# Modulation rows of a two-layer transformer formed on VectorE during the mixers, instead of on TensorE there and on VectorE in the first value stage

## The chip, the core and the metric

The kernel runs on one core of a Trainium2 chip. The metric is the device time of one execution in microseconds: the median of three executions of the kernel before is 2929.69 us, the lowest 2916.97 and the highest 2932.78.

## What is computed

Two layers over 256 context and 256 latent tokens of width 1024. In each layer six modulation vectors of length 1024 are formed for the latent stream (from c) and for the context stream (from c_ctx). They shift and scale two norms and gate two residuals:

```python
sh1, sc1, g1, sh2, sc2, g2 = jnp.split((jax.nn.silu(c) @ w_ada + b_ada)[:, None, :], 6, axis=-1)
h = rmsnorm(x, norm1_g) * (1.0 + sc1) + sh1
# four head groups on columns of h @ w_in: neighbourhood attention, mLSTM, latent attention, window attention
x = x + g1 * (jnp.concatenate([y_a, y_b, y_c, y_d], axis=-1) @ w_out)
h2 = rmsnorm(x, norm2_g) * (1.0 + sc2) + sh2
x = x + g2 * peer_ffn(h2, peer_wq, peer_keys, peer_u, peer_v)
```

`peer_ffn` routes each token to 128 of 16384 experts (8 heads, 16 each), takes gelu of its dot product with rows of `peer_u`, and sums gated rows of `peer_v`. In the second layer only the latent tokens go on after the mixers.

## The kernel before

Activations lie transposed, 128 features by 512 tokens in eight tiles. A product with a weight is three matmuls in fp32r (`mm3`, L72 to L74): the weight is loaded by SyncE's queue into a `raw` tile (2 buffers), split into a high part by ScalarE (L408) and a low part by VectorE (L412), and both parts go into `spl` tiles (10 buffers of 128x1024, taken in turn by everything that splits).

**Mixers** (`mixers`, from the start to about 455 us in layer 0 and from about 1800 to 2074 us in layer 1). TensorE's order is the order of the code. `run_units` walks over attention units, one per head and query tile of 128 tokens: 64 units in layer 0 (16 each of mLSTM, neighbourhood, latent and window attention), 32 in layer 1. For each unit it issues four transposes (`tp`, L611), the score of the unit two ahead (`sc`), then as filler some matmuls of the job list `F`, then the product with the values (`py`, L622) of the unit before, then filler again. The softmax of a unit is on VectorE and ScalarE between its score and its transposes: VectorE reduces the maximum (L567), ScalarE takes the exponential (L573), VectorE inverts the sum and scales (L577, L578). The filler jobs are the projections still needed (`naq`, `nak`, `cq`, `ckv`, `swq`, `swk`), then in layer 0 twelve jobs `ada8` to `ada19`, and, once the latent attention is done, the output projection `wo`. VectorE and ScalarE are ordered in this stretch by the framework's scheduler.

**Modulation.** Chunks 0 to 7 of layer 0 (first norm) are formed at the start on TensorE. Chunks 8 to 19 (rows 16 to 39: g1, sh2, sc2) are the twelve filler jobs (`ada_steps`): a load of 1 MB, four high and four low splits, 16 matmuls of 256 columns against `cs` (L260, L261), a copy by ScalarE (L267) and two small matmuls (L279, four records) that bring the row back. Everything else, rows 40 to 47 of layer 0 and all 48 of layer 1, is formed in the first value stage by `ada_row`: a load of 512 KB from `wadat`, two VectorE products of 128x1024 with a sum (L299, one for c, one for c_ctx, against `csb`, silu of c and c_ctx on every partition) and one small add (L300).

**Peer stage.** First norm and routing, then the `u` stage (64 pairs of blocks of experts, matmuls into `pu`), then the value stage (64 pairs, matmuls into `f`; 384 tokens in layer 0, 256 in layer 1). In layer 0 one tile of 128 tokens (`tokens_apart`) is not multiplied but gathered: GpSimd fetches rows, VectorE multiplies and adds them (L1363, L1370), spread over the `u` and the value stage. Each pair in the value stage needs four splits (L1447 on ScalarE, L1448 on VectorE) and the gated activations (L1453 to L1455). The last pair is written out by hand and begins with a lone L72 matmul.

Of the kernel before, what the change touches and what calls it, by code (L numbers as in the profile page):

```python
# [53 lines left out]
class Kernel:  # L54
# [33 lines left out]
    def build(self):  # L88
        tc, nc, A = self.tc, self.nc, self.A
        with ExitStack() as es:  # L90
# [26 lines left out]
            self.gd = [self.dram.tile([self.wd[l] // 32, 128, 128, 32], F32, name=f"gd{l}") for l in range(L)]  # L117
            self.ad = [self.dram.tile([128, 128, self.wd[l]], F32, name=f"ad{l}") for l in range(L)]
# [10 lines left out]
    def start(self):  # L129
# [15 lines left out]
        self.cs = self.sm.tile([128, KD, 128], F32R, name="cs", bufs=1)  # L145
        for half in range(2):
            zero = self.new()
            nc.gpsimd.memset(zero, 0.0)
            nc.scalar.copy(self.cs[:, 4 * half:4 * half + 4], zero.rearrange("p (a b) -> p a b", b=128))
        nc.vector.tensor_copy(self.cs[:, :, 0:2], cc)  # L150
        nc.vector.tensor_tensor(self.cs[:, :, 2:4], cc, self.cs[:, :, 0:2].bitcast(F32), op=ALU.subtract)
# [64 lines left out]
    def ada_full(self, raw, ch):  # L216
# [8 lines left out]
        row = self.sm.tile([4, 256], F32, name="adarow")  # L225
# [14 lines left out]
    def ada_parts(self, parts, ch):  # L240
        nc = self.nc
        ps = self.psc.tile([128, 512], F32, name="sc")
        for k in range(KD):
            c = slice(k % 2 * 256, k % 2 * 256 + 256)
            nc.tensor.matmul(ps[:, 0:256], self.cs[:, k, :], parts[k // 2][0][:, c], start=(k == 0), stop=False)
            nc.tensor.matmul(ps[:, 0:256], self.cs[:, k, :], parts[k // 2][1][:, c], start=False, stop=(k == KD - 1))
        self.ada_out(0, ch, ps)

    def adaload(self, l, ch):
        return self.wload(self.A["wada"][l, ch])  # L250

    def ada_steps(self, w, l, ch):

        nc = self.nc
        wh, wl = w
        if l not in self.mod:
            self.mod[l] = self.cst.tile([128, 6, KD, 2], F32, name=f"mod{l}")
        ps = self.psf.tile([128, 512], F32, name="fp")
        for k in range(KD):
            nc.tensor.matmul(ps[:, 0:256], self.cs[:, k, :], wh[:, k, :], start=(k == 0), stop=False)  # L260
            nc.tensor.matmul(ps[:, 0:256], self.cs[:, k, :], wl[:, k, :], start=False, stop=(k == KD - 1))  # L261
            yield 0.22
        self.ada_out(l, ch, ps)

    def ada_out(self, l, ch, ps):
        row = self.sm.tile([4, 256], F32, name="adarow")
# [17 lines left out]
    def ada_end(self):  # L284
        for _ in range(4):
            yield 0
        self.ada_turn()

    def ada_row(self, pool, l, n):

        nc = self.nc
        if l not in self.mod:
            self.mod[l] = self.cst.tile([128, 6, KD, 2], F32, name=f"mod{l}")
        s, k = divmod(n, KD)
        w = pool.tile([128, 1024], F32, name="adaw", bufs=2)
        nc.sync.dma_start(w, self.A["wadat"][l, n])
        for j in range(2):
            o = self.mod[l][:, s, k, j:j + 1]
            self.pin(nc.vector.scalar_tensor_tensor(self.junk, w, 1.0, self.csb[:, j], op0=ALU.mult, op1=ALU.mult, accum_out=o))  # L299
        nc.vector.tensor_add(self.mod[l][:, s, k], self.mod[l][:, s, k], self.badat[:, l, s, k:k + 1].to_broadcast([128, 2]))  # L300
# [124 lines left out]
    def mixers(self, l):  # L425
        tc, nc = self.tc, self.nc
        with ExitStack() as es:
# [37 lines left out]
            if l == 0:  # L465
# [115 lines left out]
    def run_units(self, units):  # L581
# [23 lines left out]
        for i, u in enumerate(units + [None]):  # L605
            if u is not None:
# [1142 lines left out]
```

## Time and profile before

| | |
|---|---|
| median of 3 executions | 2929.69 us |
| the profiled execution | 2918.53 us, span 2916.6 us |
| TensorE busy | 2789.8 us (96%), 18199 matmul records |
| VectorE busy | 2187.1 us (75%) |
| ScalarE busy | 1266.0 us (43%) |
| chain that ended last | TensorE 74%, VectorE 15%, DMA 3%, ScalarE 3% |
| mean granted clock | 0.981 |

A row of the profile names the line, the engine, the operation and its tiles (output<-inputs), then the count, the busy time and the mean of one in ns, then the idle time of the engine just before these instructions and what ended it. Matmuls are pipelined: the distance from one start to the next is what a matmul costs, not its shown length. PEld is TensorE's loading of weights. The granted clock is 1.00 at 2.4 GHz and 0.50 at 1.2 GHz.

### The profile page before, as it was taken

The page shows a single profiled execution, that of the slowest core. Times are in us where ns is not written, and L with a number is a line of the kernel's source. Part 1 is how long each engine was busy: PE and PEld are TensorE (multiplying, and loading weights), DVE is VectorE, ACT ScalarE, POOL GpSimd, SP SyncE. Part 2 cuts the span into 40 slices and gives each one's busy share as a digit, 9 for nine tenths or more (in the row PEclk, how much of TensorE's full clock was granted, in tenths as well). Part 3 has the DMA queues.
Part 4 walks back from the last instruction along what each step waited for, and adds up shares of the span by engine and source line. Part 5 has one row for each costly group of instructions (what it writes and reads, how often), then busy time and mean ns, then how long its engine had stood idle before and what let it go on. Part 6 is the DMA issues. An engine that isn't in the chain of part 4 may idle for free.

```text
span 2916.6 us, 47051 instructions
## 1 busy us (share of the span) xinstructions
PE 2789.8 (96%) x18199; PEld 2538.2 (87%) x18199; DVE 2187.1 (75%) x4703; ACT 1266.0 (43%) x2185; POOL 393.2 (13%) x354
## 2 busy tenths in 40 slices
PE   8999998999899997999999998999999999999998
PEld 5766777999888887999999997766899999999998
DVE  5664757679999985799999986654779767666665
ACT  5553634334344432343333334543545444444443
POOL 0110000002444433412222310000000000000000
PEclk9999999999999998999999999999999999999999
DMA  7210413326999999999999983211445766876774
GB/s 261 73 44 29 159 59 116 129 96 219 330 344 367 368 359 380 358 324 367 376 373 379 376 297 128 74 37 37 171 142 184 241 243 237 285 251 234 254 247 143
DMA packets 268752, 662.88 MB, mean 227 GB/s; under 512 B 16496, under 2 KB 146672, under 8 KB 258928
## 3 DMA queue, kind: packets, MB, share of 16 engines
q1 hardware_dynamic: 198688, 450.04, 44.1%
q0 software_dynamic: 36864, 134.23, 12.3%
q10 hardware_dynamic: 32976, 75.61, 6.8%
q8 instruction: 142, 2.33, 0.3%
q14 instruction: 82, 0.67, 0.1%
HBM read 585.37 MB, written 74.45 MB: 226 GB/s over the span
## 4 chain that ended last, share of the span: by engine, by line
PE 74%; DVE 15%; issue 4%; DMA 3%; ACT 3%; SPq 1%; POOL 0%; ACTq 0%; DVEq 0%; POOLq 0%
PE pu L72 8%; PE pu L74 8%; PE pu L73 8%; PE f L73 8%; PE f L74 7%; PE f L72 7%; PE fp L72 4%; PE fp L73 3%; PE fp L74 3%; PE py L622 3%; DVE spl L1448 2%; DVE junk L299 2%; PE pg L1328 2%; PE mm L72 2%; PE mm L73 2%
## 5 line engine op out<-in xcount | busy, mean ns | idle before, releaser
L72 PE MATMUL pu<-h2h,spl 128*128 128x384 f32 (+1 forms) x2048 | 647.9, 316 | 31.1 <-ACT spl L1396 30.0
L74 PE MATMUL pu<-h2h,spl 128*128 128x384 f32 (+1 forms) x2048 | 636.2, 312 | 10.1 <-DVE spl L1397 9.9
L73 PE MATMUL f<-wl,spl 128*128 128x384 f32 (+1 forms) x2048 | 634.0, 310 | 7.0 <-DVE wl L1455 7.0
L73 PE MATMUL pu<-h2l,spl 128*128 128x384 f32 (+1 forms) x2048 | 637.7, 311 | 0.0
L74 PE MATMUL f<-wh,spl 128*128 128x384 f32 (+1 forms) x2048 | 626.7, 309 | 0.0
L72 PE MATMUL f<-wh,spl 128*128 128x384 f32 (+1 forms) x2048 | 515.5, 311 | 9.6 <-ACT wh L1454 6.3
L1448 DVE TENSOR_TENSOR spl<-raw,spl 128x1024 fp32r<-128x1024 f32 x256 | 311.4, 1223 | 153.2 <-ACT spl L1447 151.8
L1447 ACT CAST spl<-raw 128x1024 fp32r<-128x1024 f32 x256 | 267.9, 1049 | 364.5 <-PE f L73 334.5
L72 PEld LDWEIGHTS pu<-h2h,spl 128*128 128x128 f32 x2048 | 391.5, 191 | 39.4 <-ACT spl L1396 35.6
L1396 ACT CAST spl<-raw 128x1024 fp32r<-128x1024 f32 x256 | 266.6, 1049 | 329.0 <-PE pu L73 227.3
L74 PEld LDWEIGHTS pu<-h2h,spl 128*128 128x128 f32 x2048 | 390.9, 191 | 15.3 <-DVE spl L1397 14.8
L73 PEld LDWEIGHTS f<-wl,spl 128*128 128x128 f32 x2048 | 388.9, 190 | 12.5 <-DVE wl L1455 11.1
L73 PEld LDWEIGHTS pu<-h2l,spl 128*128 128x128 f32 x2048 | 392.0, 191 | 0.4
L72 PEld LDWEIGHTS f<-wh,spl 128*128 128x128 f32 x2048 | 377.3, 190 | 15.9 <-ACT wh L1454 10.7
L1397 DVE TENSOR_TENSOR spl<-raw,spl 128x1024 fp32r<-128x1024 f32 x256 | 311.3, 1218 | 104.9 <-ACT spl L1396 94.6
L74 PEld LDWEIGHTS f<-wh,spl 128*128 128x128 f32 x2048 | 388.5, 190 | 0.0
L1414 ACT ACTIVATE act<-pu 128x384 f32<-128x384 f32 (+1 forms) x216 | 95.8, 443 | 232.3 <-PE pu L74 232.2
L412 DVE TENSOR_TENSOR spl<-raw,spl 128x512 fp32r<-128x512 f32 (+1 forms) x226 | 150.0, 699 | 58.9 <-ACT spl L408 47.9
L1454 ACT CAST wh<-va 128x384 fp32r<-128x384 f32 (+1 forms) x216 | 100.1, 467 | 185.3 <-DVE va L1453 77.6
L341 POOL TENSOR_TENSOR ms<-ms,mhalf 128x4 f32<-128x4 f32 (+1 forms) x5 | 4.8, 953 | 1300.6 <-DVE sq L339 834.0
L1357 POOL DMA_INDIRECT spl<-in_un,ix x92 | 125.0, 1359 | 393.5 <-DVE fp L1225 242.9
L408 ACT CAST spl<-raw 128x512 fp32r<-128x512 f32 (+1 forms) x226 | 130.7, 629 | 85.5 <-PE fp L73 44.2
(305 smaller groups left out, 4715.9 us busy)
## 6 DMA issues: line engine op xcount, KB each, us to landing
raw<-in_ut SPq DMA_DIRECT2D x128, 1024.0 KB, 5.3
raw<-in_v SPq DMA_DIRECT2D x128, 1024.0 KB, 5.6
adaw<-in_wadat SPq DMA_DIRECT2D x56, 512.0 KB, 7.5
ad<-act ACTq DMA_DIRECT2D x64, 384.0 KB, 5.1
gd<-gstage ACTq DMA_DIRECT2D x12, 2048.0 KB, 10.9
vg<-gd SPq DMA_DIRECT2D x32, 768.0 KB, 8.7
va<-ad SPq DMA_DIRECT2D x64, 384.0 KB, 7.6
raw<-in_win SPq DMA_DIRECT2D x22, 1024.0 KB, 4.9
```

What stands on the lines that cost most here:

```text
L72: mm(ps, ah, bh, start=first, stop=False, **kw)
L73: mm(ps, ah, bl, start=False, stop=False, **kw)
L74: mm(ps, al, bh, start=False, stop=last, **kw)
L408: return self.nc.scalar.copy(p[0][o], w[:, o])
L412: return eng.tensor_tensor(p[1][o], w[:, o], p[0][o].bitcast(F32), op=ALU.subtract)
L1357: nc.gpsimd.indirect_dma_start(r, None, tabs[which], bass.IndirectOffsetOnAxis(ix[:, s:s + 1], 0))
L1396: self.pin(nc.scalar.copy(uh, self.u[:, n % 2]), n < 3)
L1397: self.pin(nc.vector.tensor_tensor(ul, self.u[:, n % 2], uh.bitcast(F32), op=ALU.subtract), n < 3)
L1414: nc.scalar.activation(a[:, b, :w], ps[:, :w], AF.Gelu)
L1447: nc.scalar.copy(vh, v[:, b])
L1448: nc.vector.tensor_tensor(vl, v[:, b], vh.bitcast(F32), op=ALU.subtract)
L1454: nc.scalar.copy(wh[:, :w], a[:, b, :w])
```

## The change

The twelve filler jobs are gone. Rows 16 to 47 of both layers are formed on VectorE during the mixers: `run_units` takes one row after every second unit in layer 0 and after every unit in layer 1. In layer 1 only one product per row is made, since only the latent stream is left. Rows 0 to 15 of layer 1 stay in the first value stage, one after every third pair. The row's weights and the unused product go into two `spl` tiles. silu of c and c_ctx is formed once, early in the first mixers, and kept in DRAM (`csd`). To make room, `cs` moves into `s` tiles and two small pools shrink (`adarow` from 4 to 2 buffers, `dg` from 4 to 3).

```diff
+            self.csd = self.dram.tile([128, 2, 1024], F32, name="csd")
...
-        self.cs = self.sm.tile([128, KD, 128], F32R, name="cs", bufs=1)
+        self.cs = [self.new(F32R).rearrange("p (a b) -> p a b", b=128) for _ in range(2)]
...
-        row = self.sm.tile([4, 256], F32, name="adarow")
+        row = self.sm.tile([4, 256], F32, name="adarow", bufs=2)
...
+    def modulation(self, l):
+        nc = self.nc
+        nv = 2 if l == 0 else 1
+        self.csb = self.sm.tile([128, nv, 1024], F32, name="csb", bufs=1)
+        if l == 0:
+            nc.sync.dma_start(self.csb, self.A["ccb"])
+            for j in range(2):
+                sg = self.spl.tile([128, 1024], F32, name="spl")
+                nc.scalar.activation(sg, self.csb[:, j], AF.Sigmoid)
+                nc.vector.tensor_mul(self.csb[:, j], self.csb[:, j], sg)
+            nc.scalar.dma_start(self.csd, self.csb)
+        else:
+            nc.sync.dma_start(self.csb, self.csd[:, 0:1])
+        def rows():
+            for n in range(16, 48):
+                w, junk = (self.spl.tile([128, 1024], F32, name="spl") for _ in range(2))
+                self.ada_row(w, junk, l, n, nv)
+                yield
+        self.adarows = rows()
...
-            self.pin(nc.vector.scalar_tensor_tensor(self.junk, w, 1.0, self.csb[:, j], op0=ALU.mult, op1=ALU.mult, accum_out=o))
+            nc.vector.scalar_tensor_tensor(junk, w, 1.0, self.csb[:, j], op0=ALU.mult, op1=ALU.mult, accum_out=o)
...
-                for c in range(8, 20):
-                    F.add(f"ada{c}", lambda c=c: self.adaload(l, c), lambda w, c=c: self.ada_steps(w, l, c))
-                F.add("ada", None, lambda w: self.ada_end())
...
+            self.modulation(l)
             F.finish("mlg")
...
         for i, u in enumerate(units + [None]):
+            if (i + 1) * 32 // n > i * 32 // n:
+                next(self.adarows, None)
...
-                        extra = [(0, n) for n in range(40, 48)] + [(1, n) for n in range(48)]
+                        nc.sync.dma_start(self.csb, self.csd)
+                        extra = list(range(16))
...
-                        if extra:
-                            self.ada_row(self.vp, *extra.pop(0))
+                        if extra and n % 3 == 0:
+                            self.ada_row(self.vp.tile([128, 1024], F32, name="adaw", bufs=2), self.junk, 1, extra.pop(0), 2)
```

Two places of the built order matter. The first is TensorE's, in the second half of layer 0's latent attention. Before, after the score of a unit (six matmuls into `sc`), filler of the ada jobs follows:

```order
L261 MATMUL fp<-spl,cs 128x256
L611 MATMUL tp<-con,s 128x128 x4
L72 MATMUL sc<-s 128x512
L73 MATMUL sc<-s 128x512
L74 MATMUL sc<-s 128x512
L72 MATMUL sc<-s 128x512
L73 MATMUL sc<-s 128x512
L74 MATMUL sc<-s 128x512
L260 MATMUL fp<-spl,cs 128x256
L261 MATMUL fp<-spl,cs 128x256
```

With the change (lines are shifted by one) the score is followed at once by the values' product of the unit before:

```order
L722 MATMUL mm<-con,s 128x128 x4
L623 MATMUL py<-s 64x128 x2
L612 MATMUL tp<-con,s 128x128 x4
L72 MATMUL sc<-s 128x512
L73 MATMUL sc<-s 128x512
L74 MATMUL sc<-s 128x512
L72 MATMUL sc<-s 128x512
L73 MATMUL sc<-s 128x512
L74 MATMUL sc<-s 128x512
L623 MATMUL py<-s 64x128 x4
```

All 192 L260 and L261 matmuls and the 24 of L279 of the twelve jobs are gone; 13 units in a row now have no filler.

The second place is VectorE's queue in layer 0's neighbourhood attention, from the third softmax reduction on. Before:

```order
L567 TENSOR_REDUCE st<-sc 128x1
L85 TENSOR_TENSOR s<-s 128x512
L636 TENSOR_TENSOR s<-py,s 128x512
L577 RECIPROCAL st<-st 128x1
L639 CAST s<-s 128x512
L578 TENSOR_SCALAR s<-s,st 128x256
L640 TENSOR_TENSOR s<-s 128x512
L339 SCALAR_TENSOR_TENSOR s,msm<-mm,con 128x128 x4
L567 TENSOR_REDUCE st<-sc 128x1
```

With the change (L301 and L302 are the row's products and its add, `mod_213` the modulation of layer 0):

```order
L566 TENSOR_REDUCE st<-sc 128x1
L301 SCALAR_TENSOR_TENSOR spl,mod_213<-spl,csb 128x1024
L707 TENSOR_TENSOR s<-s 128x256
L301 SCALAR_TENSOR_TENSOR spl,mod_213<-spl,csb 128x1024
L302 TENSOR_TENSOR mod_213<-mod_213,badat 128x2
L85 TENSOR_TENSOR s<-s 128x512
L637 TENSOR_TENSOR s<-py,s 128x512
L301 SCALAR_TENSOR_TENSOR spl,mod_213<-spl,csb 128x1024 x2
L576 RECIPROCAL st<-st 128x1
L640 CAST s<-s 128x512
L414 TENSOR_TENSOR spl<-raw,spl 128x512 x2
L301 SCALAR_TENSOR_TENSOR spl,mod_213<-spl,csb 128x1024
```

The scheduler has not spread the rows evenly. Counted in this order for layer 0, 17 products stand between the first L954 (it weights the scores of an mLSTM unit) and the first softmax reduction, 14 between the first and the ninth reduction, 12 from there to the seventeenth, 6 to the twenty-fifth, none to the thirty-third, and 12 in the window units; the other three stand before these. In layer 1, with one product per row, 2 stand ahead of the first L954, 7 between it and the first reduction, 7 between the first and the fifth reduction, 6 from there to the ninth, and 10 behind.

## Rows read from the trace of the kernel before

**Rows 1.** The page: busy time by engine, and VectorE's tenths in 40 slices.

```profile
PE 2789.8 (96%) x18199; PEld 2538.2 (87%) x18199; DVE 2187.1 (75%) x4703; ACT 1266.0 (43%) x2185; POOL 393.2 (13%) x354
...
DVE  5664757679999985799999986654779767666665
```

**Rows 2.** Windows, value stage: span, busy (count) PE, PEld, DVE, ACT, POOL; clock, DMA.

```profile
1228.80:1776.70 547.90, 532.92 (x3024) 522.85 (x3025) 514.63 (x797) 194.41 (x260) 124.60 (x85) 1.00 0.96 347
...
1600.00:1650.00 50.00, 49.97 (x286) 49.07 (x285) 49.71 (x81) 18.12 (x25) 14.30 (x10) 1.00 1.03 373
1650.00:1700.00 50.00, 45.86 (x255) 43.51 (x254) 49.81 (x73) 15.72 (x22) 19.85 (x13) 1.00 1.03 374
```

**Rows 3.** Timeline of TensorE, same stage: start, length, instruction, count, idle before.

```profile
1764.27 1.55 PE L72 MATMUL f<-wh,spl 128*128 128x384 f32 x8
...
1772.59 1.55 PE L72 MATMUL f<-wh,spl 128*128 128x384 f32 x8
```

**Rows 4.** Groups by line, 1225 to 1775 us: VectorE's rows and ScalarE's sigmoid.

```profile
L299 DVE SCALAR_TENSOR_TENSOR junk<-adaw,csb 128x1024 f32<-128x1024 f32 x112 | 136.4, 1218 | 0.1
...
L299 DVE DVE_READ_ACCUMULATOR junk<-adaw,csb 128x1 f32 x112 | 9.2, 82 | 0.0
L300 DVE TENSOR_TENSOR mod<-mod,badat 128x2 f32<-128x2 f32 x56 | 8.7, 155 | 0.7
...
L1152 ACT ACTIVATE junk<-csb 128x1024 f32<-128x1024 f32 x2 | 2.1, 1059 | 0.5 <-DVE junk L1363 0.5
```

**Rows 5.** Groups of TensorE, 290 to 370 us: the twelve ada jobs.

```profile
L260 PE MATMUL fp<-spl,cs 128*128 128x256 f32 x96 | 27.1, 314 | 0.0
...
L611 PE MATMUL tp<-con,s 128*128 128x128 f32 x46 | 7.7, 277 | 3.1 <-ACT s L613 2.1 <-ACT st L575 0.5 <-DVE s L578 0.5
L279 PE MATMUL mm<-cmb,adarow 4*128 4x2 f32 x48 | 7.2, 251 | 0.0
```

**Rows 6.** Timeline of TensorE, end of layer 0's latent attention.

```profile
293.36 0.65 PE L622 MATMUL py<-s 128*64 128x128 f32 x4
...
303.96 0.66 PE L611 MATMUL tp<-con,s 128*128 128x128 f32 x4 [2.14 <-ACT s L613]
...
350.39 0.60 PE L279 MATMUL mm<-cmb,adarow 4*128 4x2 f32 x4
350.93 0.39 PE L260 MATMUL fp<-spl,cs 128*128 128x256 f32 x1
...
352.47 0.60 PE L611 MATMUL tp<-con,s 128*128 128x128 f32 x4
...
367.75 0.50 PE L72 MATMUL fp<-s,spl 128*128 128x512 f32 x1
```

**Rows 7.** Windows, units of layer 1 without filler.

```profile
2005.00:2010.00 5.00, 3.00 (x16) 1.81 (x14) 3.55 (x10) 0.65 (x2) 0.00 (x0) 1.00 0.00 0
2010.00:2015.00 5.00, 4.30 (x15) 3.11 (x15) 2.48 (x6) 2.40 (x6) 0.00 (x0) 0.52 0.00 0
...
2020.00:2025.00 5.00, 5.00 (x20) 3.36 (x18) 2.31 (x8) 1.54 (x4) 0.00 (x0) 0.62 0.00 0
```

**Rows 8.** Windows of VectorE alone, layer 0 mixers: span, busy (count), clock, DMA share, GB/s.

```profile
122.70:198.20 75.50, 42.21 (x175) 0.98 0.12 43
198.20:227.30 29.10, 18.95 (x59) 1.00 0.11 37
227.30:265.30 38.00, 18.10 (x44) 1.00 0.00 1
```

**Rows 9.** The same, layer 1: first to fifth, fifth to ninth reduction.

```profile
1923.70:1936.70 13.00, 10.09 (x32) 1.00 0.10 41
1936.70:1951.00 14.30, 6.44 (x17) 1.00 0.01 1
```

**Rows 10.** Timeline of TensorE, behind the first projections: its wait for ScalarE's copy.

```profile
66.05 0.50 PE L72 MATMUL fp<-s,spl 128*128 128x512 f32 x1 [0.25 <-ACT cvpad L834]
```

**Rows 11.** The page: DMA issues, KB each, median us to landing.

```profile
adaw<-in_wadat SPq DMA_DIRECT2D x56, 512.0 KB, 7.5
```

More of the change, by code (lines that the diff above doesn't have):

```diff
@@ L144, in start @@
         nc.vector.tensor_mul(cc, cc, sg)
-        self.cs = self.sm.tile([128, KD, 128], F32R, name="cs", bufs=1)
-        for half in range(2):
+        self.cs = [self.new(F32R).rearrange("p (a b) -> p a b", b=128) for _ in range(2)]
+        for half, cs in enumerate(self.cs):
             zero = self.new()
             nc.gpsimd.memset(zero, 0.0)
-            nc.scalar.copy(self.cs[:, 4 * half:4 * half + 4], zero.rearrange("p (a b) -> p a b", b=128))
-        nc.vector.tensor_copy(self.cs[:, :, 0:2], cc)
-        nc.vector.tensor_tensor(self.cs[:, :, 2:4], cc, self.cs[:, :, 0:2].bitcast(F32), op=ALU.subtract)
+            nc.scalar.copy(cs, zero.rearrange("p (a b) -> p a b", b=128))
+            c = cc[:, 4 * half:4 * half + 4]
+            nc.vector.tensor_copy(cs[:, :, 0:2], c)
+            nc.vector.tensor_tensor(cs[:, :, 2:4], c, cs[:, :, 0:2].bitcast(F32), op=ALU.subtract)
         self.hh, self.hl = [], []
@@ L244, in ada_parts @@
             c = slice(k % 2 * 256, k % 2 * 256 + 256)
-            nc.tensor.matmul(ps[:, 0:256], self.cs[:, k, :], parts[k // 2][0][:, c], start=(k == 0), stop=False)
-            nc.tensor.matmul(ps[:, 0:256], self.cs[:, k, :], parts[k // 2][1][:, c], start=False, stop=(k == KD - 1))
+            nc.tensor.matmul(ps[:, 0:256], self.cs[k // 4][:, k % 4], parts[k // 2][0][:, c], start=(k == 0), stop=False)
+            nc.tensor.matmul(ps[:, 0:256], self.cs[k // 4][:, k % 4], parts[k // 2][1][:, c], start=False, stop=(k == KD - 1))
         self.ada_out(0, ch, ps)
[L249 to L263, printed above, removed]
     def ada_out(self, l, ch, ps):
-        row = self.sm.tile([4, 256], F32, name="adarow")
+        row = self.sm.tile([4, 256], F32, name="adarow", bufs=2)
         self.nc.scalar.copy(row, ps[0:4, 0:256])
@@ L282, in ada_turn, with ada_row @@
                                 self.badat[:, l, s, k0:k0 + 2, None].to_broadcast([128, 2, 2]), op=ALU.add)
[L284 to L289, printed above, removed]
+    def modulation(self, l):
[17 more added lines that the diff above has]
+        self.adarows = rows()
+    def ada_row(self, w, junk, l, n, nv):
         nc = self.nc
@@ L293, in ada_row @@
             self.mod[l] = self.cst.tile([128, 6, KD, 2], F32, name=f"mod{l}")
+            nc.gpsimd.memset(self.mod[l], 0.0)
         s, k = divmod(n, KD)
-        w = pool.tile([128, 1024], F32, name="adaw", bufs=2)
         nc.sync.dma_start(w, self.A["wadat"][l, n])
-        for j in range(2):
+        for j in range(nv):
             o = self.mod[l][:, s, k, j:j + 1]
-            self.pin(nc.vector.scalar_tensor_tensor(self.junk, w, 1.0, self.csb[:, j], op0=ALU.mult, op1=ALU.mult, accum_out=o))
-        nc.vector.tensor_add(self.mod[l][:, s, k], self.mod[l][:, s, k], self.badat[:, l, s, k:k + 1].to_broadcast([128, 2]))
+            nc.vector.scalar_tensor_tensor(junk, w, 1.0, self.csb[:, j], op0=ALU.mult, op1=ALU.mult, accum_out=o)
+        nc.vector.tensor_add(self.mod[l][:, s, k, :nv], self.mod[l][:, s, k, :nv], self.badat[:, l, s, k:k + 1].to_broadcast([128, nv]))
     def affine(self, l, which):
@@ L946, in score @@
                     nm = self.mt[:, i, 0, d, h:h + 1]
-                    dg = self.sm.tile([128, 128], F32, name="dg", bufs=4)
+                    dg = self.sm.tile([128, 128], F32, name="dg", bufs=3)
                     mask = C_LO if d == 0 else C_UP
@@ L1691, in layout @@
     d["bada"] = _per_part(f["b_ada"].reshape(L, 6, 1024))
-    d["wada"] = _chunks(f["w_ada"][:1, :, :5120])
+    d["wada"] = _chunks(f["w_ada"][:1, :, :2048])
     d["wadat"] = np.ascontiguousarray(f["w_ada"].transpose(0, 2, 1).reshape(L, 48, 128, 1024))
```

6 lines of the change are left out of this document (removed).

## The prediction

> **What bounds the kernel now.** The page comes first: TensorE is busy for 96% of the span and VectorE for 75%, but VectorE's slices read 9 in the middle of the program and 5 to 7 elsewhere [rows 1]. So the change takes VectorE work from where it is scarcest and puts it where more is free, and it takes matmuls off the engine that is always busy. Whether this pays is read stage by stage, from windows.
>
> In the value stage of layer 0, 3024 matmuls stand between its first and the last pair, and they take 547.9 us, while VectorE is busy for 514.6 us, 94% [rows 2]. Undisturbed, 48 of them start within 8.32 us [rows 3], 0.1733 us each, so 3024 need 524.1 us. The stage loses 23.8 us. The loss is not even: with VectorE at 49.7 of 50 us one window holds 286 matmuls, which is the full rate (288), and the next one only 255 [rows 2]. VectorE is thus at the edge there, and DMA as well, with a share of 1.03.
>
> In the mixers TensorE hardly waits. In the stretch with the twelve ada jobs only 3.1 us of idle time stand before all transposes [rows 5]. Matmuls taken out there are time taken out, unless something else comes late. VectorE is the candidate: it is busy for 42.2, 18.95 and 18.1 us in 75.5, 29.1 and 38.0 us of the mLSTM and neighbourhood units [rows 8].
>
> **The sum, part by part,** in the time of the profiled execution (2918.53 us; the span is 1.9 us less).
>
> *Value stage, layer 0: -16 us.* 56 rows become 16. 40 rows are 80 products of 1.218 us, 80 sums of 0.082 and 40 adds of 0.155 [rows 4]: 110 us of VectorE's 515. It would be busy for 404 us of 524, and 40 loads of 512 KB fall away. The whole loss of 23.8 us cannot be expected back, since the full-rate windows show that the loss also has to do with when pairs and gathered rows arrive. I take two thirds, with 8 and 22 us as ends.
>
> *Latent attention, layer 0: -31.0 us of matmuls, +9.6 us of lost cover.* The 192 ada matmuls start 0.128 us apart (12 of them between 350.93 and 352.47) and the four records that bring a row back take 0.54 us (350.39 to 350.93) [rows 6]: 24.6 and 6.5 us, 31 together. The stretch from 293.36 to 367.75 us holds 74.4 us; less the 31 and the 3.1 of idle time, 40.3 us of matmuls are left for its units. The split work of these jobs, on ScalarE and VectorE, goes as well. What the filler covered comes bare: TensorE waits 2.14 us at 303.96 for a copy that stands behind the rotary work on ScalarE [rows 6], and some 3.4 us of ada matmuls ahead of it would now be waiting time too. Behind such a wait the clock can fall: in layer 1 the window at 2005 us holds only 3.0 us of matmuls, and behind it the granted clock is 0.52 and 0.62, its lower level, through units without filler [rows 7]. It stays so for about 12.4 us, 6.2 of them lost. I put 6.2 us on one such fall. The ends are no lost cover (-31) and twice as much (-12).
>
> *Rows among the mLSTM and neighbourhood units, layer 0: +12 us.* A row costs two products, two sums and an add, 2.76 us. By the counts in the order of instructions, the mLSTM units take 17 products more, 23.4 us, on 42.2 busy of 75.5: 65.6, which fits, but a softmax or weighting now stands behind 1.3 us of product more often; I take 3 us (0 to 6). Between the first and the ninth reduction 14 products add 19.3 us to 18.95 in 29.1 us [rows 8]: 38.2 us of VectorE work, 9.1 us more than there is. Nothing after it can give this back, since TensorE has all its work still to do. The score is two units ahead, which may absorb a few us, and waits inside the chain cost a few, so 9 (4 to 14). Between the ninth and the seventeenth 12 products (16.5 us) on 18.1 make 34.6 of 38.0 us: nothing.
>
> *Start and window units, layer 0: +3.6 us.* Two sigmoids of 1.06 us [rows 4] now stand on ScalarE ahead of the copies that free the first projections' banks, where TensorE already waits 0.25 us [rows 10]: 2.1 us (0 to 4). Twelve products in the window units, where VectorE has room: 1.5 us (0 to 4).
>
> *Layer 1: +8 us.* Seven products with one sum and one add (1.455 us each) are 10.2 us on top of 10.09 in 13.0 us: 20.3, so 7.3 us too much. Six more make 15.2 of the next 14.3 us [rows 9]: 0.9. The rest has room. Ends: 3 and 14.
>
> Loads in the mixers are hidden in this forecast: 512 KB each, where the DMA share is between 0.00 and 0.13 [rows 8, 9]. The memsets, the smaller pools and the transfer to DRAM I cost at nothing; they lie beside matmuls, and if the pools' cover went, a score would wait for one more GpSimd add.
>
> -16 - 31 + 9.6 + 12 + 3.6 + 8 = **-13.8 us**, 2904.7 us for an execution like the profiled one. The median of the runs shown lies 11.2 us higher, the lowest 1.6 lower, so the median of the changed kernel should be 2929.7 - 13.8, about **2916 us**. About 0.5%, 14.6 us, is what a measurement of this kernel can tell from no change: the forecast lies at that edge.
>
> **The rivals.** *VectorE's queue absorbs the rows (faster).* If the two units of distance cover the crowded stretches, the surcharges of the mixers vanish: -16 - 31 + 3.4 + 2.1, or -41.5 us, 2888 us on the scale of the median. For it: TensorE now waits for almost nothing in the mixers. Against it: 38.2 us of work do not fit into 29.1.
>
> *A row's load comes late (slower).* A row's product stands in order on VectorE; if its 512 KB have not landed, every softmax behind it waits, and TensorE behind that. Its tile is one of ten `spl` buffers, of which eight can be held by two split weights, so a load may only start once the row before is done. A landing takes 7.5 us at the median [rows 11], in a stage where DMA is full; that is the upper bound of one wait, zero the lower. Layer 0 has 63.3 us of VectorE free in the three windows of rows 8, and the rows need 59.2 of them, so from 0.2 us of wait per row the mixers grow by all that follows. With 1 us for each of some 41 rows of both layers ahead of the latent attention: -13.8 + 41, or +27 us, 2957 us.
>
> *The clock stays low (slower).* If all 13 units without filler run at the lower level seen in rows 7, their 40.3 us double: +34 on top of the 6.2 counted, in all +20 us, 2950 us. For it speak rows 7; against it the end of this very stretch in layer 0, where units already run without filler and TensorE's waits sum up to no more than 1 us [rows 5]. The Trainium skill, "TensorE: Matmul & The Clock Gate", section "HAM oscillation — how this bites in real kernels", states that repeated gaps between short bursts of matmuls bring the clock back to half rate again and again, so that each burst starts slow; by that rule this rival would be the result, whereas the trace shows one fall in layer 1 and a recovery without filler.
>
> **How the numbers follow.** The forecast as summed, -3 to -25 us, has a chance of 0.50, half of it on either side of 14.6 us. The absorbing queue has 0.22, the late loads 0.14, the low clock 0.08, and 0.06 is left for losses that just cancel the gain. So faster by more than 0.5%: 0.25 + 0.22, say 0.47; within 0.5%: 0.25 + 0.06, say 0.31; slower: 0.22. The range takes in the faster rival with a little of the value stage's upper end, down to 2880 us, and reaches into the slower ones at weaker price, up to 2945 us.
>
> **What would show it.** Right: in the value stage of layer 0, 3024 matmuls in 528 to 540 us with VectorE near 75 to 80%; no L260 and L261 lines, and the stretch without filler some 50 us long, with one fall of the clock; the first and the ninth reduction of layer 0 about 38 us apart instead of 29.1, the first and the fifth of layer 1 about 20 instead of 13.0. Wrong: waits of VectorE's products for `in_wadat`, which would point to late loads; a clock near 0.5 through all units without filler; a value stage that still takes 545 us, which would mean that VectorE was not what held it.

## The result, and the profile after

The changed kernel takes 2947.0 us (median of 15 runs, 2939.93 to 2966.42) against 2927.9 us for the kernel before on the same chips: a ratio of 1.0076, 95% interval 1.0061 to 1.0092. It is slower by 0.8%, and outside the predicted range. Eleven of the 15 runs lie between 2939.9 and 2951.3 us, four between 2959.1 and 2966.4 with a mean granted clock of 0.961 to 0.964 instead of 0.967 to 0.972. The profiled execution took 2946.8 us with a span of 2945.0, 28.4 us more than the span before. By medians the change costs 19.1 us: the profiled execution before lies 9.4 us under the median of its kernel and the one after at its median, so the table below makes the change look some 9 us dearer than it is.

Stage by stage, between the same instructions in both profiled executions (layer 0, unless layer 1 is named; `sk` is the tile of the routing's key products, behind the second norm):

| stretch | before | after | change | forecast |
|---|---|---|---|---|
| start to the first mLSTM weighting | 122.8 | 124.8 | +2.0 | +2.1 |
| to the seventeenth reduction (mLSTM, neighbourhood) | 142.6 | 166.4 | +23.8 | +12 |
| to the thirty-third (latent attention) | 96.6 | 73.1 | -23.5 | -21.4 |
| to `sk` (window units, end of the mixers, second norm) | 120.5 | 127.4 | +6.9 | +1.5 |
| `u` stage | 738.4 | 742.8 | +4.4 | 0 |
| value stage, first to last matmul into `f` | 558.7 | 562.6 | +3.9 | -16 |
| layer 1, first weighting to `sk` | 217.1 | 228.5 | +11.4 | +8 |

The other stretches change by less than 1 us each. The page shows 240 matmul records fewer and VectorE less busy by 10.6 us [rows 1], but VectorE's third and fourth slice, in the mixers, read 8 and 7 instead of 6 and 4:

```profile
PE 2781.2 (94%) x17959; PEld 2524.5 (86%) x17959; DVE 2176.5 (74%) x4701; ACT 1236.0 (42%) x2123; POOL 398.3 (14%) x355
...
DVE  6687567769999985799896556675779767666665
```

The value stage after, in windows (columns as in [rows 2]):

```profile
1242.40:1792.50 550.10, 528.79 (x3014) 521.56 (x3015) 422.36 (x594) 189.50 (x256) 114.35 (x84) 1.00 0.88 308
1342.00:1392.00 50.00, 48.16 (x275) 47.14 (x273) 47.77 (x71) 17.00 (x23) 19.31 (x14) 1.00 1.05 386
1442.00:1492.00 50.00, 44.96 (x256) 43.69 (x255) 44.17 (x65) 16.16 (x22) 19.51 (x13) 1.00 1.00 357
1642.00:1692.00 50.00, 50.00 (x290) 50.00 (x289) 26.27 (x37) 17.57 (x24) 0.00 (x0) 1.00 0.70 221
```

VectorE's busy time fell from 514.6 to 422.4 us, by 92 us where the forecast has 110, and the stage did not get shorter. (The 110 us are lengths of instructions, and these overlap: the 0.08 us in which a product's sum is read lie inside the next instruction.) It now has two halves. In the last row the stage runs at the full rate (290 matmuls) with VectorE half idle and GpSimd, which issues the gathers of the token set apart, without any. In the two rows ahead GpSimd issues 14 and 13 gathers, VectorE is busy for 44 to 48 of 50 us, DMA is at 1.00 to 1.05, and matmuls are lost. The two 50 us windows of [rows 2] differ in the same way: 286 matmuls with 10 gathers, 255 with 13, at the same VectorE and DMA load. The last sum of that token stood 483 us behind the stage's start before, and 330 us now.

VectorE in the mixers, by stretches that answer to [rows 8] (first weighting, first, ninth and seventeenth reduction), and in layer 1 from the first to the fifth and to the ninth reduction:

```profile
124.80:209.80 85.00, 63.31 (x220) 0.91 0.25 85
209.80:249.80 40.00, 34.14 (x95) 0.74 0.37 124
249.80:291.20 41.40, 30.98 (x73) 0.96 0.23 77
1940.90:1961.20 20.30, 20.00 (x58) 1.00 0.45 159
1961.20:1992.80 31.60, 19.67 (x53) 0.84 0.37 123
```

The same stretches of layer 1 before (those of [rows 9] end at the fourth and the eighth reduction):

```profile
1923.80:1939.80 16.00, 11.39 (x35) 1.00 0.08 32
1939.80:1963.90 24.10, 12.39 (x33) 1.00 0.00 1
```

The clock column is what is new: 0.91, 0.74 and 0.96 in layer 0 where it was 0.98, 1.00 and 1.00 [rows 8]. What that costs shows in TensorE's windows from the first weighting to the thirteenth reduction, before and after, with the same 527 records. Before:

```profile
122.80:244.10 121.30, 118.82 (x527) 76.24 (x528) 70.70 (x260) 67.51 (x167) 13.10 (x27) 0.99 0.10 35
```

With the change:

```profile
124.80:270.00 145.20, 132.36 (x527) 82.40 (x527) 114.12 (x354) 68.15 (x167) 21.52 (x29) 0.87 0.28 92
```

Of 23.9 us, 13.5 are the same matmuls running longer (118.8 to 132.4 us busy) and 10.4 are idle time.

### The profile page after: what moved, and what is told of

Read it like the earlier page. It is cut to its first block, busy times and chain, and to the rows that moved or that the text cites. A ratio compares the mean times of both kernels' runs of the same rounds, so it can differ in the third digit from the quotient of the medians.

```text
span 2945.0 us, 46539 instructions
## 1 busy us (share of the span) xinstructions
PE 2781.2 (94%) x17959; PEld 2524.5 (86%) x17959; DVE 2176.5 (74%) x4701; ACT 1236.0 (42%) x2123; POOL 398.3 (14%) x355
## 4 chain that ended last, share of the span: by engine, by line
PE 67%; DVE 14%; issue 11%; DMA 5%; ACT 2%; POOL 0%; SPq 0%; ACTq 0%; another core or an unknown queue 0%; DVEq 0%; POOLq 0%
PE f L73 8%; PE pu L72 8%; PE f L74 8%; PE pu L74 8%; PE f L72 8%; PE pu L73 8%; PE fp L72 3%; PE fp L73 2%; PE fp L74 2%; PE pg L1325 2%; PE mm L73 2%; PE mm L72 2%; PE mm L74 2%; DVE junk L1360 1%; DVE spl L1394 1%
## 5 line engine op out<-in xcount | busy, mean ns | idle before, releaser
L72 PE MATMUL f<-wh,spl 128*128 128x384 f32 (+1 forms) x2048 | 512.0, 310 | 15.8 <-ACT wh L1451 12.6
L1445 DVE TENSOR_TENSOR spl<-raw,spl 128x1024 fp32r<-128x1024 f32 x256 | 313.1, 1225 | 240.6 <-ACT spl L1444 238.3
L74 PEld LDWEIGHTS pu<-h2h,spl 128*128 128x128 f32 x2048 | 392.4, 192 | 13.5 <-DVE spl L1394 12.7
L72 PE MATMUL fp<-s,spl 128*128 128x512 f32 (+1 forms) x416 | 166.6, 401 | 2.4 <-ACT cvpad L835 1.7
L73 PE MATMUL fp<-s,spl 128*128 128x512 f32 (+1 forms) x416 | 152.6, 367 | 1.8 <-DVE s L641 1.8
```

The costliest lines, as they stand in the source:

```text
L72: mm(ps, ah, bh, start=first, stop=False, **kw)
L73: mm(ps, ah, bl, start=False, stop=False, **kw)
L74: mm(ps, al, bh, start=False, stop=last, **kw)
L1445: nc.vector.tensor_tensor(vl, v[:, b], vh.bitcast(F32), op=ALU.subtract)
```

## The experiments

Two questions stood open: why the value stage kept its length with so much of VectorE's work gone, and what made the mixers longer. "Built order" is the order of instructions on an engine that the framework's scheduler settles on; the counts below are taken from the traces, which show it. All stage times are of one profiled execution per kernel.

**The value stage: who sets the pace.** In the kernel before, each row's product was pinned behind the VectorE instruction written before it, one row per pair, and this also held the gathered token's products and sums to the pace of the code. The change unpinned the rows. Of the gathered token's 256 products and sums this many stand ahead of VectorE's split 32, 48 and so on (of the stage's 128, two per pair; the expectations below count pairs, of 64):

| gathered products and sums done | split 32 | 48 | 64 | 80 | 96 |
|---|---|---|---|---|---|
| before | 185 | 197 | 211 | 223 | 235 |
| after | 200 | 220 | 239 | 256 | 256 |
| `pinrow` | 191 | 203 | 215 | 228 | 238 |
| `pace` | 189 | 201 | 213 | 225 | 237 |
| `fewrows` | 191 | 203 | 216 | 227 | 238 |
| `pacefast` | 200 | 219 | 238 | 256 | 256 |

`pinrow`, the pin given back to the rows of the value stage:

```diff
-            nc.vector.scalar_tensor_tensor(junk, w, 1.0, self.csb[:, j], op0=ALU.mult, op1=ALU.mult, accum_out=o)
+            self.pin(nc.vector.scalar_tensor_tensor(junk, w, 1.0, self.csb[:, j], op0=ALU.mult, op1=ALU.mult, accum_out=o), n < 16)
```

> Edit: the changed kernel, with the products of the 16 rows in the first value stage kept behind the VectorE instruction written before them, as all rows there were before the change. Nothing else. Theory A (run-ahead): the value stage of layer 0 stayed at 562.6 us because the gathered token's rows, which the pinned products held to the pace of the code, now run ahead and fill VectorE and DMA in its first half. In the built order all 256 gathered products stand ahead of split 40 of 128 in the changed kernel, and ahead of split 56 here. So the stage takes 530 to 540 us, the whole kernel about 2947 - 25 = 2922 us, and TensorE's loss is spread thin. Rival B (VectorE never held the stage; DMA, buffers or TensorE's feed do): 555 to 565 us, and 2940 to 2950 us in all. Mixers: within 1 us of the changed kernel by both.

Measured: value stage 559.7 us, median 2952.2 us, ratio 1.0117 (1.0086 to 1.0147). The pace came back and the time did not. `pace`, the gathered work itself pinned (`paced` is set from the first value stage on):

```diff
-            nc.vector.scalar_tensor_tensor(junk, r, 1.0, ht, op0=ALU.mult, op1=ALU.mult, accum_out=dots[:, s:s + 1])
+            self.pin(nc.vector.scalar_tensor_tensor(junk, r, 1.0, ht, op0=ALU.mult, op1=ALU.mult, accum_out=dots[:, s:s + 1]), self.paced)
...
-                nc.vector.scalar_tensor_tensor(self.facc, r, wt[:, s:s + 1], self.facc, op0=ALU.mult, op1=ALU.add)
+                self.pin(nc.vector.scalar_tensor_tensor(self.facc, r, wt[:, s:s + 1], self.facc, op0=ALU.mult, op1=ALU.add), self.paced)
```

> Edit: the changed kernel, with the gathered token's own products and sums (L1360, L1367) kept in the order of the code during the value stages, and the rows left free. It holds the pace from the other side. Theory A: as with the pinned rows, value stage of layer 0 530 to 540 us, the kernel about 2922 us. If only the rows' own place mattered and not the gathered token's: 555 to 563 us and no gain. Rival B: 555 to 565 us.

Measured: value stage 546.1 us, median 2932.3 us, ratio 1.0046 (1.0020 to 1.0071). Two later kernels with the same value stage, `pinall` and `late`, repeat it with 546.5 and 547.1 us. `pinrow` and `pace` differ in one thing that VectorE's waits show (total in us, times, longest). In `pinrow`:

```profile
DVE spl L1445 <- ACT spl L1444: 59.4, 42, 3.9
DVE facc L1367 <- DMA row<-in_vn,ix: 32.4, 20, 3.7
```

There VectorE stands still 20 times for a gathered row that has not landed, and what is queued behind it is late; `pace` has no such line in its list of waits. In the kernel before, its sums waited 0.0 us. The traces show a difference that fits. `pace` takes products and sums in turn almost throughout. `pinrow` takes two or three products in a row and then as many sums, while GpSimd gathers for both in turn and into four buffers. From the issue of a gather to the sum that uses its row the median is 9.3 us in `pinrow`, 13.9 before and 21.7 in `pace`. No run changes this order alone, so that it is the cause is not shown.

`fewrows`, the kernel before with 40 rows left out of the value stage:

```diff
-                        extra = [(0, n) for n in range(40, 48)] + [(1, n) for n in range(48)]
+                        extra = [(1, n) for n in range(16)]
...
-                        if extra:
+                        if extra and n % 3 == 0:
```

> Edit: the kernel before, with 40 of the 56 rows of the first value stage left out (rows 40 to 47 of layer 0 and 16 to 47 of layer 1 are zeros, so the second norm's result is gated to nothing) and the 16 left spread over every third pair, still pinned. It shows what the value stage gives for the change's edit when the mixers and the pacing are as before. Theory A: 530 to 540 us instead of 558.7, the kernel about 2905 us. Rival B: 553 to 560 us, 2920 to 2930 us.

Measured: 567.6 us, 8.9 us longer than with all 56 rows, the kernel 2932.0 us. So the change's edit of this stage is worth nothing on its own, with the pin as without it; again VectorE waits 31.2 us for gathered rows (median from gather to sum 10.1 us). Both theories were short of it: the gain came where rows were removed and the gathered work itself was kept in the order of the code.

`pacefast` spreads the same work, in order, over 36 pairs instead of 58:

```diff
-                        rows_to(PHASE1 + (256 - PHASE1) * n // 58 if n < 58 else 300)
+                        rows_to(PHASE1 + (256 - PHASE1) * n // 36 if n < 36 else 300)
```

> Edit: the paced kernel with the gathered token's work spread over 36 pairs of the value stage instead of 58, in the order of the code. The built order has 204, 223, 242 and 256 of its products ahead of splits 16, 24, 32 and 40, the same as the changed kernel within one. If the run-ahead itself costs (the same work in fewer pairs crowds VectorE and DMA): value stage of layer 0 at 558 to 565 us, as with the change, against 546.1 when spread over 58. If it is the scheduler's disorder that costs and not the pace: 543 to 550 us.

Measured: 565.8 us. The run-ahead itself costs some 20 us, in order or not. To see which resource is crowded then, each was taken away in turn. `fast8` keeps the transfers (the sum is cut in the same way):

```diff
+            c = slice(0, 8 if self.paced else 1024)
+            self.pin(nc.vector.scalar_tensor_tensor(junk[:, c], r[:, c], 1.0, ht[:, c], op0=ALU.mult, op1=ALU.mult, accum_out=dots[:, s:s + 1]), self.paced)
```

`fastht` keeps VectorE's work:

```diff
+            if self.paced:
+                return ht
             r = self.row_tile()
```

> Edit: the kernel with the gathered token's work in 36 pairs (value stage of layer 0 565.8 us, against 546.1 in 58 pairs), with its VectorE products and sums in the value stage cut to 8 of 1024 columns; the rows are still fetched (the token gathered apart gets another result). Some 140 us of VectorE work go, all transfers stay. If VectorE is what is crowded there: 530 to 540 us. If the transfers are (DMA share 1.05 in those windows): 558 to 566 us. Both in part: 541 to 557.

> Edit: the same kernel (36 pairs) with the gathered token's products and sums whole, but in the value stage they read a tile that is already there, so that no row is fetched (the token gathered apart gets another result). Some 64 MB/1024 = 0.5 MB per row go from DMA, all VectorE work stays. If the transfers are what is crowded: 530 to 540 us. If VectorE is: 558 to 566 us.

Measured: 546.4 and 547.8 us. Either relief alone brings back nearly all of the 19.7 us between `pacefast` and `pace`. A window of `pace` (VectorE is the third busy time, GpSimd with its gathers the fifth):

```profile
1443.00:1493.00 50.00, 50.00 (x290) 50.00 (x289) 42.08 (x63) 18.07 (x26) 16.08 (x10) 1.00 0.96 337
```

Of `pacefast`:

```profile
1335.00:1385.00 50.00, 46.42 (x262) 44.82 (x261) 46.02 (x67) 16.93 (x24) 18.01 (x14) 1.00 1.02 370
```

Of `fast8`:

```profile
1445.00:1495.00 50.00, 50.00 (x291) 50.00 (x290) 33.14 (x68) 17.97 (x25) 15.94 (x14) 1.00 1.05 385
```

Of `fastht`:

```profile
1434.00:1484.00 50.00, 50.00 (x290) 50.00 (x289) 47.35 (x69) 17.57 (x24) 0.00 (x0) 1.00 0.77 242
```

Full transfers with VectorE at 33 of 50 us run at the full rate, and so does VectorE at 47 of 50 with DMA at 0.77. At 14 gathers in 50 us only both together lose matmuls. The shares alone do not decide it: the kernel before, with 10 gathers, has 286 matmuls at 49.7 of 50 and 1.03 [rows 2]. How the gathers and VectorE's work hinder each other is not shown.

**The mixers: work, loads or clock.** `norows` leaves out the 32 rows per layer in the mixers; `oneload` makes the products without loading; `loadsonly` loads, but multiplies 8 columns. `norows`:

```diff
-                next(self.adarows, None)
+                pass
```

`oneload`, which also skips the loads of rows 16 to 47:

```diff
-            nc.vector.scalar_tensor_tensor(junk, w, 1.0, self.csb[:, j], op0=ALU.mult, op1=ALU.mult, accum_out=o)
+            src, dst = (w, junk) if n < 16 else (self.csb[:, 0], (w, junk)[j])
+            nc.vector.scalar_tensor_tensor(dst, src, 1.0, self.csb[:, j], op0=ALU.mult, op1=ALU.mult, accum_out=o)
```

`loadsonly`:

```diff
+            c = slice(0, 1024 if n < 16 else 8)
+            nc.vector.scalar_tensor_tensor(junk[:, c], w[:, c], 1.0, self.csb[:, j, c], op0=ALU.mult, op1=ALU.mult, accum_out=o)
```

> Edit: the changed kernel without the 32 rows per layer in the mixers (their modulation values are zeros: g1, sh2, sc2, g2 of both layers). It shows what the mixers take when only the twelve jobs of TensorE are gone. From the first weighting to sk the mixers of layer 0 took 359.7 us before and 366.9 with the change. If the rows' VectorE work and loads make the surcharge: 359.7 - 31 + 5 to 10 us of lost cover = 334 to 339 us. If waits behind missing cover or the clock make it: 345 us or more. Layer 1: 217 us as before if the rows make its 11 us, 228 if not. The value stage of layer 0 stays at 555 to 565 us by either theory, with the gathered rows still running ahead.

> Edit: the changed kernel; the 32 rows per layer in the mixers keep their products and adds, but no weights are loaded for them (each product reads the resident silu tile twice, so rows 16 to 47 hold other values). From the first weighting to the thirteenth reduction of layer 0 the profiled executions show 121.3 us before, 145.2 with the change and 125.3 without rows; from the first to the thirteenth reduction of layer 1 66.2, 79.8 and 66.4. Theory W (the products' own time on VectorE, 2.76 and 1.46 us a row, makes the surcharge): 140 to 146 and 77 to 80 us. Theory L (VectorE waits for late loads): 125 to 130 and 66 to 70 us. Both at once: between.

> Edit: the changed kernel; the 32 rows per layer in the mixers are loaded as before, but each product covers 8 of the 1024 columns (rows 16 to 47 hold other values), so that a row waits for its load but costs VectorE little. Theory W: 125 to 129 us in the stretch of layer 0 and 66 to 69 in that of layer 1. Theory L: 138 to 146 and 75 to 80 us.

Measured, TensorE's and VectorE's windows from the first weighting to the thirteenth reduction of layer 0. `norows`:

```profile
124.90:250.20 125.30, 122.83 (x527) 78.42 (x528) 70.54 (x260) 67.66 (x167) 13.55 (x28) 0.95 0.09 30
```

`oneload`:

```profile
125.00:290.80 165.80, 139.74 (x527) 85.91 (x528) 122.05 (x370) 69.46 (x167) 20.55 (x28) 0.82 0.07 23
```

`loadsonly`:

```profile
125.80:253.00 127.20, 123.41 (x532) 78.65 (x532) 75.78 (x358) 67.25 (x165) 13.81 (x28) 0.96 0.33 112
```

The products cost, the loads do not: with loads and hardly any work the stretch is 1.9 us longer than without rows. Without loads it is 20.6 us longer than the changed kernel, which neither theory had: the loads had held the rows back. In the built order 48 of the 64 row products are ahead of the ninth reduction there, 34 in the changed kernel and none without rows (an expectation below counts four or five more in each). From the first weighting to that reduction the times are 149.1, 125.0 and 108.6 us. `loadsonly`, which also has 34 there, but short ones, takes 108.3. `norows` came to 347.4 us for layer 0's mixers, not 334 to 339, because of the clock (0.92 in the mLSTM units, 0.86 and 0.63 in the eight units ahead of the thirty-third reduction), and to 212.5 us in layer 1.

`pinall` is `pace` with the rows of the mixers pinned to their places in the code (22 products ahead of the ninth reduction):

```diff
-            nc.vector.scalar_tensor_tensor(junk, w, 1.0, self.csb[:, j], op0=ALU.mult, op1=ALU.mult, accum_out=o)
+            self.pin(nc.vector.scalar_tensor_tensor(junk, w, 1.0, self.csb[:, j], op0=ALU.mult, op1=ALU.mult, accum_out=o), n >= 16)
```

> Edit: the paced kernel, and the products of the mixers' rows kept behind the VectorE instruction written before them, so that they stand where the code puts them: one row after every second unit in layer 0, one after every unit in layer 1. In the built order the products ahead of the ninth reduction of layer 0 number 26 of all such products, against 38 in the changed kernel, 4 without rows and 53 in the kernel without loads; the time from the first weighting to that reduction was 125.0, 108.6 and 149.1 us in the latter three. Theory W (VectorE's work ahead of that point sets the time): about 116 us, by the line through these, and 146 - 8 = 138 us or less to the thirteenth; layer 1 from 79.8 to about 72; in all some 15 us below the paced kernel, 2917 us. If order in itself costs (VectorE waits in its queue for a row's load): 125 us or more, 2932 us or more.

The same window of `pinall`:

```profile
124.30:254.70 130.40, 124.19 (x527) 78.36 (x528) 95.18 (x316) 65.90 (x163) 20.21 (x30) 0.94 0.23 75
```

To the ninth reduction it took 113.4 us, to the thirteenth 130.4, 14.8 us less than the change, and 74.9 us in layer 1 from the first to the thirteenth (79.8 with the change): what the count of products says. In all it gave nothing that can be told from `pace`: 2937.4 us, ratio 1.0036 (1.0017 to 1.0054). Its profiled execution, the fastest of nine, lost part of the early gain again. Layer 0's mixers took 360.2 us in all (366.9 with the change), with the clock at 0.50 between the twenty-ninth and the thirty-third reduction, and layer 1's 230.7 (228.5). `late` moves the rows into the second half of the units, each loaded one ahead and pinned, on top of `pace`:

```diff
-            if (i + 1) * 32 // n > i * 32 // n:
+            for _ in range(64 // n if i >= n // 2 - 1 else 0):
```

> Edit: the paced kernel (gathered token's work in the order of the code in the value stages), and the rows of the mixers begin only with the second half of the units (latent and window attention: one row a unit in layer 0, two in layer 1), each loaded one row ahead and its product kept behind what is written before it on VectorE. From the first weighting to sk the mixers of layer 0 took 359.7 us before, 366.9 with the change, 347.4 without rows; layer 1 217.1, 228.5, 212.5. If VectorE's room decides (some 99 us are free in layer 0 behind the seventeenth reduction, the rows need 88): 347 to 355 and 213 to 220 us, value stage of layer 0 546 us, and about 2932 - 21 = 2911 us in all. If waits for loads or a low clock take the place: 360 us or more, 225 or more, and 2925 us or more.

Measured: layer 0's mixers 370.1 us, layer 1's 230.3, ratio 1.0049 (1.0026 to 1.0072). The early stretch is back to 121.9 us, and the later ones pay instead: 82.4 us for the latent attention (73.1 with the change), with the clock at 0.50 between the twenty-ninth and the thirty-third reduction, and 144.6 us from there to `sk` (127.4).

**The clock.** The changed kernel once more, unedited:

> The changed kernel once more, without an edit, for a second profiled execution. The u stage of layer 0 took 738.4 us before and 742.8 with the change, with no edit in it, and 735 to 753 us in the kernels since, longer where the granted clock is lower. If that comes from the built order: within 1 us of 742.8 again. If it varies from execution to execution: it may be anywhere from 735 to 753. The mixers (366.9 and 228.5 us) and the value stage (562.6) within 2 us of the first profile if their causes lie in the order.

Measured: 2957.8 us. Layer 0's mixers (365.5 us) and the value stage (562.7) came again, so their causes lie in the order. The `u` stage took 746.1 us, and layer 1's mixers 235.7 instead of 228.5, which was not expected. There the stretch from the thirteenth to the twenty-first reduction took 48.2 us instead of 41.2, with the same 208 records. The second execution's window:

```profile
2022.80:2071.00 48.20, 45.38 (x208) 32.47 (x209) 23.61 (x64) 16.16 (x38) 0.00 (x0) 0.79 0.14 48
```

The first one's:

```profile
2020.70:2061.90 41.20, 36.77 (x208) 26.52 (x209) 23.39 (x64) 15.94 (x38) 0.00 (x0) 1.00 0.16 57
```

The low clock of the units without filler varies in the same way. `pacefast` and `fast8` have the same order on TensorE, VectorE and ScalarE in layer 0's mixers. From the twenty-fifth to the thirty-third reduction `pacefast` shows:

```profile
337.50:360.50 23.00, 22.71 (x120) 15.40 (x121) 10.87 (x35) 9.21 (x25) 0.00 (x0) 0.94 0.01 1
```

And `fast8`:

```profile
338.30:375.90 37.60, 37.60 (x118) 24.73 (x119) 10.94 (x34) 9.77 (x25) 0.00 (x0) 0.50 0.00 1
```

In both the clock falls 13 to 18 us ahead of this stretch, among waits of TensorE of up to 2.3 and 3.0 us. In one it is back at 2.4 GHz 3 us into the stretch, in the other it stays at 1.2 GHz to the end of these units and 11 us on: 14.6 us for nothing but the clock. The fast case is the usual one here. Seven profiled executions have the changed kernel's order in layer 0's mixers. Six of them (the change twice, `pinrow`, `pace`, `pacefast`, `fastht`) took 23.0 to 23.4 us in this stretch; `fast8` alone took 37.6.

**A version that beats both.** `bpace` keeps the twelve jobs on TensorE, paces the gathered work as in `pace`, and drops the product of rows 16 to 47 of layer 1 that nobody reads (80 products instead of 112). `bpace62` spreads the gathered work over 62 pairs.

```diff
-        for j in range(2):
+        nv = 2 if l == 0 or n < 16 else 1
+        for j in range(nv):
```

```diff
-                        rows_to(PHASE1 + (256 - PHASE1) * n // 58 if n < 58 else 300)
+                        rows_to(PHASE1 + (256 - PHASE1) * n // 62 if n < 62 else 300)
```

> Edit: the kernel before (twelve jobs on TensorE in the mixers), with the gathered token's products and sums kept in the order of the code in the value stages, and of the rows 16 to 47 of layer 1 only the product for the latent stream, which alone is used later: 80 products instead of 112 in the value stage. If pacing is what the stage lacked, with VectorE some 15% freer: 542 to 550 us instead of 558.7, and about 2915 us in all. If the number of rows decides, as the run-ahead theory had it at first: 548 to 556 us. If the pinned rows hold VectorE behind gathered rows that have not landed, as with the pinned and the fewer rows: 558 to 567 us, 2925 us or more.

> Edit: the kernel before with paced gathered rows and single products for layer 1's later rows (2914 us, value stage 552.5 us), and the gathered token's work spread over 62 pairs of the value stage instead of 58. If the spread decides: 549 to 552 us and 2911 to 2914 us in all. If the last rows then come too late for the end of the stage: 555 us or more.

Measured: value stage 552.5 and 551.2 us; medians 2914.5 and 2914.3 us, ratios to the kernel before 0.9966 (0.9949 to 0.9982) and 0.9947 (0.9928 to 0.9965). The two can't be told apart. `mixed` forms only rows 16 to 39 in layer 0's mixers:

```diff
-            for n in range(16, 48):
+            for n in range(16, 40):
...
-            if (i + 1) * 32 // n > i * 32 // n:
+            if self.l == 0 and (i + 1) * 24 // n > i * 24 // n:
```

> Edit: a mixture. Rows 16 to 39 of layer 0, which the twelve TensorE jobs made before, are formed on VectorE in the mixers (24 rows over 64 units, kept in the order of the code); the others are in the value stage of layer 0, paced over 62 pairs, with a single product for rows 16 to 47 of layer 1; the mixers of layer 1 are as before. Layer 0 from the first weighting to sk: 352 to 360 us (pinned rows in place 360.2, without rows 347.4, before 359.7). Layer 1: 217 us. Value stage 549 to 553 us. In all 2905 to 2914 us if the mixers gain what 8 rows fewer suggest, 2915 us or more, no better than the paced kernel with the twelve jobs (2914 us), if the low clock of the units without filler takes it back.

Measured: 2926.4 us, ratio 0.9986 (0.9974 to 0.9997). Layer 0's mixers took 367.4 us, with the clock at 0.50 from the twenty-fifth to the thirty-third reduction; the value stage 549.1. Taking the jobs off TensorE did not pay in any version: what they cost, the versions without them lose to the clock or to VectorE's queue.

## Why the prediction was wrong

**Value stage, -16 us: the step that failed most,** 19.9 of the 42.2 us between the forecast and the profiled execution. It took the freed 110 us as room, and left where the gathered work stands as it was. That work was held in place by the very rows that went: ahead of split 64 it grew from 211 to 239 of 256. With it paced the stage gains 12.6 us (546.1 against 558.7), within the ends of 8 and 22. The forecast priced the resource and missed the order. Its own sentence that DMA is at the edge too was the hint: `fast8` and `fastht` show that relief of either brings the matmuls back. By the prediction's own sign, a stage of 545 us or more, VectorE would not have been what held it; `fast8` shows that it was one of the two things that did, once the gathered work ran ahead.

**mLSTM and neighbourhood units, +12 us: mis-sized, measured 23.8.** The mechanism held in part: products ahead of a reduction set the time, and loads did not. But the surcharge was worked out as VectorE's excess alone, and a product was priced too high: it starts 1.15 us ahead of the next instruction, its sum inside that one's time, not 1.30:

```profile
222.29 1.23 DVE L301 SCALAR_TENSOR_TENSOR spl<-spl,csb 128x1024 f32<-128x1024 f32 x1
223.44 0.09 DVE L301 DVE_READ_ACCUMULATOR spl<-spl,csb 128x1 f32 x1
```

Between the first and the ninth reduction VectorE was busy for 34.1 of 40.0 us, so it was no longer full where the forecast has it as the bound; the stretch grew by 10.9 us all the same. "Fits" was no assurance: the mLSTM units, with VectorE at 63.3 of 85.0 us, grew by 9.5 us, not 3, of which 4.1 stand in `norows` as well, without any row and with the clock at 0.92. And of the 23.9 us to the thirteenth reduction 13.5 came from the clock behind TensorE's waits, a term that the sum had at one place only.

**Latent attention, -21.4 us: right (-23.5), and not certain.** Six of seven executions of this order gain 22.9 to 23.8 us there. `fast8`, the seventh, gains 9.2 us (96.6 to 87.4), outside the stated ends; to that extent a single execution that agrees is luck. Lost cover is not 9.6 us but, against the 31 us of matmuls, 7.5 or 21.8, as the clock goes.

**Window units, +1.5 us: measured +6.9.** VectorE had room on average, but rows stood in bunches: between the forty-first and the last reduction the change takes 42.4 us, and 34.6, as before, with the rows pinned in place (`pinall`). Spreading them does not remove the cost, though: the whole stretch to `sk` is 128.4 us in `pinall`, and 124.4 in `norows`, 3.9 above the kernel before without any row. **Start, +2.1: right** (+2.0). **Layer 1, +8 us: 11.4**, within its ends, and 18.6 in the second execution, outside them. The prediction's "fifth" and "ninth" reduction there were the fourth and the eighth. To the true fifth it took 20.3 instead of 16.0 us (+4.3, forecast 7.3), from there to the ninth 31.6 instead of 24.1 (+7.5, forecast 0.9, with a clock of 0.84 behind it), so the sum was near and its terms were not. **`u` stage, 0: +4.4 and +7.7** in two executions, with a clock of 0.97 instead of 0.98; TensorE's busy time grew by 4.2 us in the first. It is not shown that the change causes this, since it varies with the order unchanged.

**The rivals.** VectorE's absorbing queue did not come. The late loads were priced right in kind only: row products wait 36.0 us in all, 24 times, but 5.3 us of them, 6 times, between 125 and 270 us, in the stretch that grew most, and `loadsonly` clears them:

```profile
DVE spl L301 <- DMA spl<-in_wadat: 36.0, 24, 5.3
DVE spl L301 <- DMA spl<-in_wadat: 5.3, 6, 1.3
```

The low clock, given 0.08, was real in one other execution of this order (`fast8`) and in other kernels without filler, and part of the result in other stages. The Trainium skill, "TensorE: Matmul & The Clock Gate", section "HAM oscillation — how this bites in real kernels", says that waits between short bursts of matmuls bring the half rate back. The traces agree that it comes back (0.50 for 20.5 us in `pacefast`, for 61.4 us in `fast8`); how long it stays differs between executions of one order.

## What to carry to other kernels

Before costing freed time on an engine, ask what the removed instructions held in place: a pinned instruction also paced what the scheduler may float, and the freed room was filled with work that could have waited. Take TensorE's filler away only where no wait stands ahead of it, and price a wait with the clock behind it. A product that nobody reads, and work that runs ahead of its need, are cheaper to fix than work is to move.

## What the runs showed of the hardware

The granted clock makes one and the same order differ by 14.6 us in one stretch and by 7.0 us in another from execution to execution. With the gathered work in 36 pairs, VectorE and the DMA engines together cost TensorE 18 to 19 us of 566, and next to nothing when either was relieved (`fast8`, `fastht`); by which way is not shown. The busy shares alone do not tell it: with fewer gathers the kernel before held 286 matmuls in 50 us at 49.7 us of VectorE and a DMA share of 1.03. A VectorE product of 128x1024 with its sum cost 1.15 us of the queue, less than the 1.30 us that the two lengths add up to.
